# Feed-forward matmuls that stream a chunk's 256 columns in five other orders

## The chip, the cores and the metric

The kernel runs on one core of one Trainium2 chip, as one launch. The metric is device time in microseconds (us) for the whole launch, the median of the runs shown. Nothing else runs beside it: there is no second core, and the host does no arithmetic.

## The reference, cut to what matters

The reference is two transformer blocks in a row on 256 tokens of width 1024. Three of its parts are gated feed-forward layers with 2816 hidden features; the change is made in these three, so only they are shown:

```python
def swiglu(x, w_gate, w_up, w_down):
    return (jax.nn.silu(x @ w_gate) * (x @ w_up)) @ w_down

# first block
f = swiglu(rms_norm(h, ffn1_pre_g[i]), ffn1_w_gate[i], ffn1_w_up[i], ffn1_w_down[i])
h = h + 0.5 * rms_norm(f, ffn1_post_g[i])
...
f = swiglu(rms_norm(h, ffn2_pre_g[i]), ffn2_w_gate[i], ffn2_w_up[i], ffn2_w_down[i])
h = h + 0.5 * rms_norm(f, ffn2_post_g[i])
...
# second block
gate, up = jnp.split(hf @ w_ffn_in[l], 2, axis=-1)
x = x + (jax.nn.silu(gate) * up) @ w_ffn_out[l]
```

Between them stand a mixer with neighbourhood attention and pooling, a per-layer gate, a mixer with stick-breaking attention and a convolution, and attention to a memory. All data are float32.

## The kernel before, in words

Activations lie with features on the 128 partitions and the 256 tokens along the row, so a "chunk" is a tile of 128 features by 256 tokens. Every weight matrix is cut into blocks of 128 x 128, and all blocks come from HBM in one stream, in the order in which they are used: a unit of eight blocks is one DMA (tile `raw`, L63) on the queue of SP.

To come near float32, each operand is split into a high part and a low part of the type float32r: ScalarE writes the high part of a unit (`wh`, L90) and VectorE the low part (`wl`, L101), four units ahead of their use. Activations are split the same way, into two tiles: `xH` and `xL` for the input of a layer, `aH` and `aL` for the hidden features. A product of a block with a chunk is then three matmuls into one PSUM bank, all issued at L184 by way of `mm3`:

```python
self.mm(b, out, w[0], x[0])
self.mm(b, out, w[1], x[0])
self.mm(b, out, w[0], x[1], stop=stop)
```

The weights are the stationary operand (128 columns, loaded by a LDWEIGHTS row of PEld before each matmul), the chunk is the moving operand (256 columns, streamed in a row), and the sum is written to 256 neighbouring words of a PSUM bank.

A feed-forward layer (`ffn`) has two stages. The first makes 22 hidden chunks `m`, each from eight input chunks for the gate and eight for the up half: the first four `m` together, input chunk by input chunk, the other 18 one after the other. The gate half and the up half of one `m` lie side by side in one bank; `evac` multiplies them by the norm's factor (z, L414), takes silu on ScalarE (L415), multiplies (L418) and splits the product into `aH` (ScalarE, L421) and `aL` (VectorE, L424). The second stage makes eight output chunks, each a sum over the 22 hidden chunks. So each of the three layers has 18 x 16 = 288 blocks in the part of the first stage that the change touches, and 8 x 22 = 176 blocks in the second, three matmuls each. What the engines do in which order is written out by hand: `after(n, fn)` and `tick` put small pieces of work of the other engines behind matmuls, and each engine runs its list in order.

Some other lines are spoken of below. `mem_v_task` and `first_group` swap the operands (`mm3t`): there a chunk's 128 tokens are the stationary operand and weights are the moving one, 256 or 512 columns of them, and the first two of the three matmuls have the same stationary operand. L688 (`scaled`, first mixer) reads a bank and the factor with a step of four words and writes in a row; L930 does the same job in the second mixer with everything in a row. L286 (`high_x`) writes `xH`; in the eight calls of the first join it writes with a step of four words (`columns`), elsewhere in a row.

Of the kernel before, what the change touches and what calls it, by code (L numbers as in the profile page):

```python
# [15 lines left out]
P = 128  # L16
# [33 lines left out]
class Stream:  # L50
    """Weight blocks [128, 128] in the order in which the tensor engine takes them."""
# [19 lines left out]
    def split_now(self, u, cuts=(UB,)):  # L71
        """Both parts of unit u, for the start, when nothing else is to be done."""
# [43 lines left out]
def columns(a):  # L116
    """A view of 256 tokens in the order of the grid's columns as one in the order of its rows."""
    return a.rearrange("p (c r) -> p r c", r=GR)


class Bank:
    def __init__(self, t):
        self.t = t
        self.started = False


class Net:
# [63 lines left out]

    def mm3t(self, b, out, x, w, stop=False):
        self.mm(b, out, x[0], w[0])
        self.mm(b, out, x[0], w[1])
        self.mm(b, out, x[1], w[0], stop=stop)

    def proj(self, b, sub, name, m, ks, x):
        """One chunk of 128 outputs, features on partitions."""
        for i, k in enumerate(ks):
            w = self.ws.take(name, k, m)  # L200
            self.mm3(b, b.t[:, sub], w, (x[0][:, k], x[1][:, k]), stop=i == len(ks) - 1)
# [5 lines left out]
    def setup(self):  # L207
# [3 lines left out]
        self.xH = b.tile([P, DC, T], F32R, name="xH")  # L211
        self.xL = b.tile([P, DC, T], F32R, name="xL")
# [33 lines left out]
    def stat(self, parts):  # L246
        """1 / rms of the tokens: parts are pieces [128, 256] of partial sums of squares."""
# [19 lines left out]
    def bcast(self, r):  # L267
        """1 / rms on every partition, in PSUM."""
# [28 lines left out]
    def squares(self, acc, in_, first, scale=1.0):  # L297
        """acc += (scale * in_)^2, chunk by chunk."""
# [8 lines left out]
    def sq_pair(self, j):  # L307
        """Squares of the stream's chunks 2j and 2j + 1."""
# [15 lines left out]
    def post_chunk(self, c, src, gain, scale=1.0):  # L324
        """Chunk c of a branch that is normed before it joins the stream."""
        nc = self.nc
        if c == 0:
            self.acc = self.new_acc()
        self.squares(self.acc, src, c == 0, scale)
        nc.scalar.activation(out=self.fg[:, c], in_=src, func=AF.Copy, scale=gain(c))  # L330

    def join(self, gain, fills, scale=None):
        """h += normed branch; then the next norm's operands, chunk by chunk."""
# [7 lines left out]
        x = (self.xH, self.xL)  # L341
# [43 lines left out]
    def add_chunk(self, c, src, gain, x):  # L385
        """h += branch, with the next norm's operands."""
# [7 lines left out]
    def add_pair(self, j, src, gain, x):  # L394
        """h += branch for two chunks of one bank, with the next norm's operands."""
# [8 lines left out]
    def ffn(self, gate, up, down, on_chunk, nk=4):  # L404
        nc = self.nc
        x = (self.xH, self.xL)
        with self.tc.tile_pool(name="ffn", bufs=1, reuse_waits="tile") as fp:
            self.fp = fp
            aH = fp.tile([P, FC, T], F32R, name="aH")
            aL = fp.tile([P, FC, T], F32R, name="aL")  # L410

            def evac(m, b):
                z = fp.tile([P, 2, T], F32, tag="z", name="z", bufs=6)
                nc.vector.tensor_tensor(out=z, in0=b.t, in1=self.row(rs), op=ALU.mult)  # L414
# [16 lines left out]
            for k in range(DC):  # L431
                for m in range(nk):
                    for sub, (name, off) in enumerate((gate, up)):
                        w = self.ws.take(name, k, off + m)
                        self.mm3(bs[m], bs[m].t[:, sub], w, (x[0][:, k], x[1][:, k]), stop=k == DC - 1)
# [4 lines left out]
            for m in range(nk):  # L440
                evac(m, bs[m])
            for m in range(nk, FC):
                b = self.bank()
                for sub, (name, off) in enumerate((gate, up)):
                    self.proj(b, sub, name, off + m, range(DC), x)
                    if sub == 1:
                        evac(m, b)
                    self.tick()
            for c in range(DC):
                b = self.bank()  # L450
                for k in range(FC):
# [4 lines left out]
                on_chunk(c, b.t[:, 0])  # L456

# [21 lines left out]
    def mem_k_task(self, c):  # L479
        nc = self.nc  # L480
        b = self.bank()
        for k in range(DC):
            w = self.ws.take("w_mem_kv_2", k, c)
            self.mm3(b, b.t[:, 0], w, (self.mH[:, k], self.mL[:, k]), stop=k == DC - 1)
# [29 lines left out]
    def ple_task(self, j):  # L514
        nc = self.nc
        b = self.bank()
        for sub in range(2):
            for k in range(2):
                w = self.ws.take("ple_w_proj", k, 2 * j + sub)
                self.mm3(b, b.t[:, sub], w, (self.pH[:, k], self.pL[:, k]), stop=k == 1)  # L520
# [6 lines left out]
    def first_group(self, win, vc, qc, kc):  # L527
        """Values (tokens on partitions) and the first two chunks of queries and keys, input chunk by chunk."""
        x = (self.xH, self.xL)
        vb = [self.bank() for _ in range(2)]  # L530
        qb = [self.bank() for _ in range(2)]
        for k in range(DC):
# [5 lines left out]
            for i in range(2):  # L538
                for sub, off in enumerate((qc, kc)):
                    w = self.ws.take(win, k, off + i)  # L540
                    self.mm3(qb[i], qb[i].t[:, sub], w, (x[0][:, k], x[1][:, k]), stop=k == DC - 1)
# [6 lines left out]
    def pair_task(self, win, m0, m1, evac):  # L548
        """Two output chunks in one bank; a generator of half tasks."""
        x = (self.xH, self.xL)  # L550
# [17 lines left out]
    def clear_pads(self, qz, vz):  # L568
        """The halves of queries and values that belong to a pair's other head."""
# [25 lines left out]
    def merge(self, tile, na, nb, oa, ob, tg, x, tanh_now):  # L595
        """merged = sigmoid(ga) * branch a + sigmoid(gb) * branch b, split, into x."""
# [25 lines left out]
    def from_merged(self, name, m, on_chunk):  # L622
        bs = [self.bank() for _ in range(2)]
        for ks in (range(DC - 2), (DC - 2, DC - 1)):
            for c in range(4):
                for k in ks:
                    w = self.ws.take(name, k, c)
                    self.mm3(bs[c // 2], bs[c // 2].t[:, c % 2], w, (m[0][:, k], m[1][:, k]), stop=k == DC - 1)
# [13 lines left out]
    def mixer1(self, fills):  # L642
        nc, tc, d = self.nc, self.tc, self.d
        with tc.tile_pool(name="mix1", bufs=1, reuse_waits="tile") as mp:
# [9 lines left out]
            oH = mp.tile([P, 4, T], F32R, name="oH")  # L654
            oL = mp.tile([P, 4, T], F32R, name="oL")
            yH = mp.tile([P, 4, T], F32R, name="yH")
            yL = mp.tile([P, 4, T], F32R, name="yL")
# [78 lines left out]
            def pool_mm(g):  # L736
                b = self.flat_bank()
                w = self.ws.take("pool_w", g, 0)
                self.mm3(b, b.t[:, 0:T], w, (yH[:, g], yL[:, g]), stop=True)
# [82 lines left out]
            m = (self.xH, self.xL)  # L822
# [589 lines left out]
```

## Time and profile before

| what | value |
|---|---|
| device time, median of 2 runs | 1041.83 us (1041.7 to 1041.95) |
| span of the profiled execution, first to last instruction | 1040.2 us |
| granted TensorE clock, mean over the span | 0.998 of full speed |
| matmul rows / weight-load rows | 8606 / 8606 |
| VectorE busy, ScalarE busy | 709.6 us (68%), 545.7 us (52%) |
| HBM traffic over the span | 183 GB/s |

The span is the time of the profiled execution that a trace can show; it lies 1.6 us under the median of the timed runs, for what comes before the first and after the last instruction. A matmul's row begins when it begins to be streamed and its length is modelled and covers the neighbour's start; so what one matmul costs in a dense stretch is read from the distance between the starts of neighbouring rows, not from the rows' lengths.

### The profile page before, as it was taken

What the parts mean: (1) busy time and instruction counts of PE and PEld (TensorE: products, weight loads), DVE (VectorE), ACT (ScalarE), POOL (GpSimd) and SP (SyncE); (2) the same over time, 40 slices, a digit from 0 to 9 for tenths busy, and PEclk for the clock granted to TensorE, in tenths of its full rate; (3) what the DMA queues carried; (4) which work ended last, traced back from release to release, by engine and by line L of the source; (5) the groups of instructions that cost most, each with busy time, mean ns of one, the idle gap of its engine ahead of it and who ended that gap; (6) DMA issues with size and microseconds to landing.
All of it is one profiled execution on the core that took longest, in us unless ns stands there. A gap on an engine that the chain in (4) does not pass through costs nothing.

```text
span 1040.2 us, 20720 instructions
## 1 busy us (share of the span) xinstructions
PE 1030.7 (99%) x8606; PEld 1022.6 (98%) x8606; DVE 709.6 (68%) x1062; ACT 545.7 (52%) x857; POOL 44.0 (4%) x73
## 2 busy tenths in 40 slices
PE   9999999999999999999999999999999999999997
PEld 8999999999999999999999999999999999999996
DVE  7777754587858677666447776886678677666642
ACT  7655544464644555454446565465556555544431
POOL 0100000120000110000000111000001000000000
PEclk9999999999999999999999999999999999999999
DMA  8765564555545655556555666454566346555541
GB/s 287 244 214 181 194 215 171 181 190 185 194 151 166 229 179 193 184 191 190 196 167 177 195 201 194 159 168 157 160 222 226 110 139 219 187 199 182 178 147 42
DMA packets 55023, 191.50 MB, mean 184 GB/s; under 512 B 6400, under 2 KB 7936, under 8 KB 54928
## 3 DMA queue, kind: packets, MB, share of 16 engines
q1 hardware_dynamic: 52992, 184.37, 53.6%
q0 software_dynamic: 1936, 5.80, 1.8%
q8 instruction: 67, 1.10, 0.4%
q14 instruction: 28, 0.23, 0.1%
HBM read 187.00 MB, written 3.15 MB: 183 GB/s over the span
## 4 chain that ended last, share of the span: by engine, by line
PE 81%; issue 16%; DMA 1%; DVE 1%; SPq 0%; POOL 0%; POOLq 0%; DVEq 0%; ACT 0%
PE mm L184 77%; PE at L184 3%; DMA raw<-ws 1%; PE at L839 1%; DMA hg<-gx 0%; DVE sqp L315 0%; POOL r L264 0%; DVE wl L79 0%; SPq L63 0%; DVE wl L101 0%; DVE xL L290 0%; DVE fg L1323 0%; POOLq L1405 0%; DVEq L1405 0%; ACT wh L78 0%
## 5 line engine op out<-in xcount | busy, mean ns | idle before, releaser
L184 PE MATMUL mm<-xH,wh 128*128 128x256 f32 x1760 | 494.9, 281 | 0.0
L184 PE MATMUL mm<-xH,wl 128*128 128x256 f32 x1760 | 492.2, 280 | 0.8 <-DVE wl L79 0.4
L184 PE MATMUL mm<-xL,wh 128*128 128x256 f32 x1760 | 491.4, 279 | 0.0
L101 DVE TENSOR_TENSOR wl<-raw,wh 128x1024 fp32r<-128x1024 f32 x340 | 405.8, 1218 | 22.0 <-ACT wh L90 7.4
L90 ACT CAST wh<-raw 128x1024 fp32r<-128x1024 f32 x340 | 350.2, 1046 | 53.0 <-PE mm L184 33.5
L184 PEld LDWEIGHTS mm<-xH,wl 128*128 128x128 f32 x1760 | 331.2, 188 | 2.6 <-DVE wl L79 1.4
L184 PEld LDWEIGHTS mm<-xH,wh 128*128 128x128 f32 x1760 | 331.3, 188 | 1.6 <-ACT wh L78 0.8
L184 PEld LDWEIGHTS mm<-xL,wh 128*128 128x128 f32 x1760 | 331.1, 188 | 0.0
L184 PE MATMUL mm<-aH,wh 128*128 128x256 f32 x528 | 148.9, 282 | 0.0
L184 PE MATMUL mm<-aL,wh 128*128 128x256 f32 x528 | 148.2, 281 | 0.0
L184 PE MATMUL mm<-aH,wl 128*128 128x256 f32 x528 | 148.2, 281 | 0.0
L415 ACT ACTIVATE z<-z 128x256 f32<-128x256 f32 x66 | 27.2, 418 | 145.6 <-DVE z L414 145.5
L184 PEld LDWEIGHTS mm<-aH,wl 128*128 128x128 f32 x528 | 99.6, 189 | 0.0
L184 PEld LDWEIGHTS mm<-aH,wh 128*128 128x128 f32 x528 | 99.6, 189 | 0.0
L184 PEld LDWEIGHTS mm<-aL,wh 128*128 128x128 f32 x528 | 99.5, 189 | 0.0
L414 DVE TENSOR_TENSOR z<-mm,rs 128x512 f32<-128x512 f32 x66 | 44.7, 689 | 77.5 <-PE mm L184 71.8
L305 DVE TENSOR_TENSOR acc<-acc,sq 128x256 f32<-128x256 f32 x27 | 11.5, 425 | 65.0 <-ACT sq L304 64.9
L264 POOL TENSOR_TENSOR r<-v,mhalf 128x2 f32<-128x2 f32 x13 | 17.6, 1355 | 685.7 <-DVE v L262 685.7
L286 ACT ACTIVATE xH<-hg 128x256 fp32r<-128x256 f32 x48 | 23.6, 543 | 31.9 <-DVE hg L355 22.0
L304 ACT ACTIVATE sq<-mm 128x256 f32<-128x256 f32 x21 | 8.2, 390 | 53.8 <-PE mm L184 53.8
L418 DVE TENSOR_TENSOR z<-z 128x256 f32<-128x256 f32 x66 | 27.2, 423 | 8.7 <-ACT z L415 7.5
L424 DVE TENSOR_TENSOR aL<-z,aH 128x256 fp32r<-128x256 f32 x66 | 26.6, 415 | 0.0
(238 smaller groups left out, 1225.9 us busy)
## 6 DMA issues: line engine op xcount, KB each, us to landing
raw<-ws SPq DMA_DIRECT2D x340, 512.0 KB, 4.1
raw<-ws SPq DMA_DIRECT2D x9, 256.0 KB, 6.0
ub<-ub SPq DMA_DIRECT2D x8, 160.0 KB, 2.9
mraw<-memT POOLq DMA_DIRECT2D x8, 128.0 KB, 3.7
kd<-kv POOLq DMA_DIRECT2D x8, 128.0 KB, 3.0
vd<-kv POOLq DMA_DIRECT2D x4, 256.0 KB, 3.4
kv<-kd POOLq DMA_DIRECT2D x4, 256.0 KB, 6.2
kv<-vd POOLq DMA_DIRECT2D x4, 256.0 KB, 7.1
```

Source lines behind the costliest of these rows:

```text
L90: self.nc.scalar.copy(out=h, in_=self.R[self.nhigh])
L101: self.nc.vector.tensor_tensor(out=l, in0=self.R.pop(u), in1=self.H[u].bitcast(F32), op=ALU.subtract)
L184: self.nc.tensor.matmul(out, lhsT, rhs, start=not b.started, stop=stop, skip_group_check=True)
L264: nc.gpsimd.tensor_tensor(out=r, in0=v, in1=self.mhalf, op=ALU.pow)
L286: self.nc.scalar.activation(out=self.ordered(x[0][:, c]), in_=self.rows(self.h[:, c]), func=AF.Copy, scale=gain(c))
L304: nc.scalar.activation(out=s, in_=in_, func=AF.Square, scale=scale)
L305: nc.vector.tensor_tensor(out=acc, in0=acc, in1=s, op=ALU.add)
L414: nc.vector.tensor_tensor(out=z, in0=b.t, in1=self.row(rs), op=ALU.mult)
L415: nc.scalar.activation(out=z[:, 0], in_=z[:, 0], func=AF.Silu)
L418: nc.vector.tensor_tensor(out=z[:, 0], in0=z[:, 0], in1=z[:, 1], op=ALU.mult)
L424: nc.vector.tensor_tensor(out=aL[:, m], in0=z[:, 0], in1=aH[:, m].bitcast(F32), op=ALU.subtract)
L839: self.nc.tensor.transpose(b.t[:, i * T + t * P:i * T + (t + 1) * P], u[:, t, kt * P:(kt + 1) * P], self.ident)
```

## The change

The high and the low part of an activation now lie in one tile, chunk by chunk: `Split` wraps a tile `[128, chunks, 2, 256]`, and `at(k)` gives the high part, the low part and both in a row (512 columns). All other stages use it with the same three matmuls as before. In the feed-forward layers, from the fifth `m` on and in the whole second stage, the matmuls are issued in other orders:

| layer, stage | order | matmuls |
|---|---|---|
| first, stage 1 | `wide`: high weights over 512 columns in a row (high and low part), low weights over 256; a bank per half | 288 of 512 and 288 of 256 columns |
| first, stage 2 | `(8, 2)`: pairs of words, the next pair 64 bytes on | 528 |
| second, stage 1 | `same`: high weights on the high part, high weights on the low part, then the low weights | 864 |
| second, stage 2 | `(8, 16)`: pieces of 16 words (64 bytes), the next 512 bytes on | 528 |
| third, stage 1 | `(2, 16)`: pieces of 16 words (64 bytes), every second one first | 864 |
| third, stage 2 | `(2, 8)`: pieces of 8 words (32 bytes), every second one first | 528 |

The pieces are taken in the same order from the chunk and in the PSUM bank, so each sum lands where it did. In `wide` the high half of the bank holds two of the three products and the second half the third, so they have to be added: `join2` copies one half to SBUF on ScalarE (L452) and adds the other on VectorE (L453), 36 times each; `evac` then reads `z` from SBUF instead of the bank (L456). Nothing is left out of the computation.

```diff
+class Split:
+    def __init__(self, t):
+        self.t = t
+    def __getitem__(self, i):
+        return self.t[:, :, i]
+    def at(self, k):
+        return self.t[:, k, 0], self.t[:, k, 1], self.t[:, k]
...
+    def mm3o(self, b, out, w, x, order, stop=False):
+        if order == "same":
+            self.mm(b, out, w[0], x[0])
+            self.mm(b, out, w[0], x[1])
+            self.mm(b, out, w[1], x[0], stop=stop)
+            return
+        f = lambda a: a.rearrange("p (a b c) -> p b a c", b=order[0], c=order[1])
+        self.mm3(b, f(out), w, (f(x[0]), f(x[1])), stop=stop)
+
+    def mm2(self, b, w, x, stop=False):
+        self.mm(b, b.t, w[0], x[2])
+        self.mm(b, b.t[:, 0], w[1], x[0], stop=stop)
...
+            def join2(z, b):
+                nc.scalar.copy(out=z, in_=b.t[:, 1])
+                nc.vector.tensor_tensor(out=z, in0=b.t[:, 0], in1=z, op=ALU.add)
...
             for m in range(nk, FC):
-                b = self.bank()
+                z = zt()
                 for sub, (name, off) in enumerate((gate, up)):
-                    self.proj(b, sub, name, off + m, range(DC), x)
-                    if sub == 1:
-                        evac(m, b)
+                    if o1 == "wide":
+                        b = self.bank()
+                        self.wide(b, name, off + m, range(DC), x)
+                        join2(z[:, sub], b)
+                        if sub == 1:
+                            evac(m, z, z)
+                    else:
+                        b = b if sub else self.bank()
+                        for k in range(DC):
+                            self.mm3o(b, b.t[:, sub], self.ws.take(name, k, off + m), x.at(k), o1, stop=k == DC - 1)
...
                 for k in range(FC):
                     w = self.ws.take(down, k, c)
-                    self.mm3(b, b.t[:, 0], w, (aH[:, k], aL[:, k]), stop=k == FC - 1)
+                    if two:
+                        self.mm2(b, w, a.at(k), stop=k == FC - 1)
+                    else:
+                        self.mm3o(b, b.t[:, 0], w, a.at(k), "same" if o2 == "wide" else o2, stop=k == FC - 1)
...
-        self.ffn(("ffn1_w_gate", 0), ("ffn1_w_up", 0), "ffn1_w_down", lambda c, s: self.post_chunk(c, s, gp1))
+        self.ffn(("ffn1_w_gate", 0), ("ffn1_w_up", 0), "ffn1_w_down", lambda c, s, t: self.post_chunk(c, s, gp1, more=t), "wide", (8, 2))
...
+        self.ffn(("ffn2_w_gate", 0), ("ffn2_w_up", 0), "ffn2_w_down", lambda c, s, t: self.post_chunk(c, s, gp2, more=t), "same", (8, 16))
...
+        self.ffn(("w_ffn_in_2", 0), ("w_ffn_in_2", FC), "w_ffn_out_2", self.last_chunk, (2, 16), (2, 8))
```

The case `o2 == "wide"` is in the code but not called, so the added argument of `post_chunk` and `last_chunk` is always empty.

Two places show what moved. The first is TensorE at the end of stage 1 and the beginning of stage 2 of the first layer, before; `x` and `a` are the chunks, `mm` a PSUM bank, and the last figures are the columns of a matmul:

```order
L184 MATMUL mm_1681<-xH_78,wh_1545 128x256
L184 MATMUL mm_1681<-xH_78,wl_1578 128x256
L184 MATMUL mm_1681<-xL_79,wh_1545 128x256
L184 MATMUL mm_1748<-aH_188,wh_1576 128x256
L184 MATMUL mm_1748<-aH_188,wl_1619 128x256
L184 MATMUL mm_1748<-aL_189,wh_1576 128x256
```

The same place now, where three figures behind the 128 are the nested counts of the columns:

```order
L197 MATMUL mm_1518<-x_78,wh_1378 128x512
L197 MATMUL mm_1518<-x_78,wl_1406 128x256
L197 MATMUL mm_1547<-a_186,wh_1404 128x8x16x2
L197 MATMUL mm_1547<-a_186,wl_1441 128x8x16x2
L197 MATMUL mm_1547<-a_186,wh_1404 128x8x16x2 x2
```

A block of stage 1 is two matmuls instead of three, and one of stage 2 is still three, with the columns cut in pairs; the last row joins the third matmul of one block and the first of the next.

The second place is VectorE in stage 1 of the first layer, before:

```order
L101 TENSOR_TENSOR wl_790<-raw_639,wh_750 128x1024
L414 TENSOR_TENSOR z_816<-mm_747,rs_446 128x512
L424 TENSOR_TENSOR aL_189<-z_742,aH_188 128x256
L418 TENSOR_TENSOR z_816<-z_816 128x256
L101 TENSOR_TENSOR wl_826<-raw_681,wh_788 128x1024
L101 TENSOR_TENSOR wl_857<-raw_712,wh_824 128x1024
L414 TENSOR_TENSOR z_883<-mm_821,rs_446 128x512
```

And now:

```order
L101 TENSOR_TENSOR wl_650<-raw_524,wh_612 128x1024
L453 TENSOR_TENSOR z_644<-mm_645,z_644 128x256
L101 TENSOR_TENSOR wl_676<-raw_554,wh_648 128x1024
L453 TENSOR_TENSOR z_644<-mm_671,z_644 128x256
L456 TENSOR_TENSOR z_644<-z_644,rs_443 128x512
L466 TENSOR_TENSOR a_186<-z_582,a_186 128x256
L460 TENSOR_TENSOR z_644<-z_644 128x256
L101 TENSOR_TENSOR wl_706<-raw_584,wh_674 128x1024
L453 TENSOR_TENSOR z_700<-mm_701,z_700 128x256
```

Between two splits of weight units there now stands an addition (L453) that waits for the ScalarE copy of the same half and so for the bank's last matmul; the other work of a chunk is what it was.

## Rows read from the trace of the kernel before

**Rows 1.** The page's totals by engine, and TensorE and its clock in 40 slices

```profile
PE 1030.7 (99%) x8606; PEld 1022.6 (98%) x8606; DVE 709.6 (68%) x1062; ACT 545.7 (52%) x857; POOL 44.0 (4%) x73
...
PE   9999999999999999999999999999999999999997
...
PEclk9999999999999999999999999999999999999999
```

**Rows 2.** Costliest groups: line, engine, operation, count | busy us, mean ns | idle before

```profile
L184 PE MATMUL mm<-xH,wl 128*128 128x256 f32 x1760 | 492.2, 280 | 0.8 <-DVE wl L79 0.4 <-DVE wl L101 0.3
...
L184 PE MATMUL mm<-aH,wh 128*128 128x256 f32 x528 | 148.9, 282 | 0.0
```

**Rows 3.** Timeline of TensorE, first layer, stage 1: start and length, 28 rows

```profile
99.78 0.28 PE L184 MATMUL mm<-xH,wh 128*128 128x256 f32 x1
...
102.93 0.28 PE L184 MATMUL mm<-xH,wh 128*128 128x256 f32 x1
```

**Rows 4.** The same in the first layer's stage 2, 22 rows

```profile
170.03 0.28 PE L184 MATMUL mm<-aH,wl 128*128 128x256 f32 x1
...
172.52 0.28 PE L184 MATMUL mm<-aH,wl 128*128 128x256 f32 x1
```

**Rows 5.** The same in the first mixer, six matmuls of 512 columns

```profile
212.65 0.39 PE L184 MATMUL mm<-wh,xH 128*128 128x512 f32 x1
...
213.81 0.40 PE L184 MATMUL mm<-wh,xL 128*128 128x512 f32 x1
214.05 0.28 PE L184 MATMUL mm<-xH,wh 128*128 128x256 f32 x1
```

**Rows 6.** The same in the memory's values: two matmuls with one stationary operand

```profile
600.71 0.28 PE L184 MATMUL mm<-wh,mH 128*128 128x256 f32 x1
600.83 0.28 PE L184 MATMUL mm<-wl,mH 128*128 128x256 f32 x1
...
602.87 0.28 PE L184 MATMUL mm<-wh,mH 128*128 128x256 f32 x1
```

**Rows 7.** Weight loads of those matmuls: ns min/median/max, first and last start

```profile
L184 PEld LDWEIGHTS mm<-wh,mH x64: 187/188/193, 585.6 to 609.2; 128*128 128x128 f32 x64
...
L184 PEld LDWEIGHTS mm<-wl,mH x64: 187/188/193, 585.7 to 609.4; 128*128 128x128 f32 x64
```

**Rows 8.** VectorE groups by shape: in a row, and (L688) with a step of four words

```profile
L101 DVE TENSOR_TENSOR wl<-raw,wh 128x1024 fp32r<-128x1024 f32 x340 | 405.8, 1218 | 22.0 <-ACT wh L90 7.4 <-issue 7.1 <-PE mm L184 7.1
...
L688 DVE TENSOR_TENSOR tg<-mm,rs 128x512 f32<-128x512 f32 x4 | 4.3, 1077 | 8.9 <-PE mm L184 8.9
...
L566 DVE TENSOR_TENSOR kT<-mm,rs 128x256 f32<-128x256 f32 x8 | 3.4, 424 | 0.1
...
L930 DVE TENSOR_TENSOR tg<-mm,rs 128x512 f32<-128x512 f32 x4 | 2.8, 691 | 8.8 <-PE mm L184 8.8
```

**Rows 9.** ScalarE's writes of xH: ns min/median/max, first and last start

```profile
L286 ACT ACTIVATE xH<-hg x48: 493/509/772, 3.2 to 848.7; 128x256 fp32r<-128x256 f32 x48
L603 ACT ACTIVATE xH<-u x8: 417/417/419, 312.8 to 334.5; 128x256 fp32r<-128x256 f32 x8
...
L1076 ACT CAST xH<-kv x4: 614/618/620, 790.5 to 802.4; 128x512 fp32r<-128x512 f32 x4
```

**Rows 10.** A ScalarE copy of 256 columns out of PSUM

```profile
L276 ACT COPY rs<-at 128x256 f32<-128x256 f32 x6 | 2.2, 372 | 17.4 <-PE at L184 17.4
```

**Rows 11.** Stretches: us, busy PE, PEld, DVE, ACT, POOL with counts, clock, DMA, GB/s

```profile
40.00:140.00 100.00, 100.00 (x858) 100.00 (x858) 73.80 (x110) 53.49 (x89) 3.40 (x6) 1.00 0.61 197
145.00:207.00 62.00, 62.00 (x520) 61.64 (x519) 30.89 (x39) 26.12 (x37) 2.73 (x3) 1.00 0.53 180
385.00:500.00 115.00, 115.00 (x987) 115.00 (x986) 78.45 (x108) 57.80 (x90) 1.08 (x2) 1.00 0.59 191
```

More of the change, by code (lines that the diff above doesn't have):

```diff
@@ L190, in mm3, with wide @@
         self.mm(b, out, w[0], x[1], stop=stop)
+    def mm3o(self, b, out, w, x, order, stop=False):
[9 more added lines that the diff above has]
+        self.mm(b, b.t[:, 0], w[1], x[0], stop=stop)
+    def wide(self, b, name, m, ks, x):
+        for i, k in enumerate(ks):
+            self.mm2(b, self.ws.take(name, k, m), x.at(k), stop=i == len(ks) - 1)
     def mm3t(self, b, out, x, w, stop=False):
@@ L322, in new_acc, with post_chunk @@
         return self.tmp.tile([P, T], F32, tag="acc", name="acc", bufs=2)
-    def post_chunk(self, c, src, gain, scale=1.0):
+    def post_chunk(self, c, src, gain, scale=1.0, more=None):
         nc = self.nc
@@ L328, in post_chunk @@
             self.acc = self.new_acc()
+        if more is not None:
+            nc.scalar.copy(out=self.fg[:, c], in_=more)
+            nc.vector.tensor_tensor(out=self.fg[:, c], in0=src, in1=self.fg[:, c], op=ALU.add)
+            src = self.fg[:, c]
         self.squares(self.acc, src, c == 0, scale)
@@ L340, in join @@
         h, fg = self.h, self.fg
-        x = (self.xH, self.xL)
+        x = self.x
         def mul(lo, n):
@@ L401, in add_pair, with ffn, zt, evac @@
         self.after(3, lambda: self.sq_pair(j))
-    def ffn(self, gate, up, down, on_chunk, nk=4):
+    def ffn(self, gate, up, down, on_chunk, o1, o2, nk=4):
         nc = self.nc
-        x = (self.xH, self.xL)
+        x = self.x
         with self.tc.tile_pool(name="ffn", bufs=1, reuse_waits="tile") as fp:
             self.fp = fp
[L409 to L414, printed above, removed]
+            a = Split(fp.tile([P, FC, 2, T], F32R, name="a"))
+            aH, aL = a[0], a[1]
+            def zt():
+                return fp.tile([P, 2, T], F32, tag="z", name="z", bufs=6)
+            def join2(z, b):
+                nc.scalar.copy(out=z, in_=b.t[:, 1])
+                nc.vector.tensor_tensor(out=z, in0=b.t[:, 0], in1=z, op=ALU.add)
+            def evac(m, z, src):
+                nc.vector.tensor_tensor(out=z, in0=src, in1=self.row(rs), op=ALU.mult)
                 nc.scalar.activation(out=z[:, 0], in_=z[:, 0], func=AF.Silu)
@@ L450, in ffn @@
                 b = self.bank()
+                two = c < DC - 1 and o2 == "wide"
                 for k in range(FC):
                     w = self.ws.take(down, k, c)
-                    self.mm3(b, b.t[:, 0], w, (aH[:, k], aL[:, k]), stop=k == FC - 1)
+                    if two:
+                        self.mm2(b, w, a.at(k), stop=k == FC - 1)
+                    else:
+                        self.mm3o(b, b.t[:, 0], w, a.at(k), "same" if o2 == "wide" else o2, stop=k == FC - 1)
                     if k % 8 == 4:
                         self.tick()
-                on_chunk(c, b.t[:, 0])
+                on_chunk(c, b.t[:, 0], b.t[:, 1] if two else None)
     def mem_prep_chunk(self, c):
@@ L653, in mixer1 @@
             tg2 = mp.tile([P, 4, 2, T], F32, name="tg2")
[L654 to L657, printed above, removed]
+            o = Split(mp.tile([P, 4, 2, T], F32R, name="o"))
+            y = Split(mp.tile([P, 4, 2, T], F32R, name="y"))
+            oH, oL, yH, yL = o[0], o[1], y[0], y[1]
             tg1 = self.fg.rearrange("p (a b) t -> p a b t", b=2)
@@ L1151, in trans @@
                 b = self.transposed(st[h])
-                pH, pL = (mp.tile([P, 2, T], F32R, tag="p" + i, name="p" + i, bufs=n) for i, n in (("H", 2), ("L", 1)))
+                p = Split(mp.tile([P, 2, 2, T], F32R, tag="p", name="p", bufs=2))
+                pH, pL = p[0], p[1]
                 bt = b.t.rearrange("p (a t) -> p a t", a=2)
@@ L1217, in memory, with last_chunk @@
             outk((6, 7), True)
-    def last_chunk(self, c, src):
+    def last_chunk(self, c, src, more):
         nc = self.nc
@@ L1223, in last_chunk @@
         nc.vector.tensor_tensor(out=h[:, c], in0=src, in1=h[:, c], op=ALU.add)
+        if more is not None:
+            nc.vector.tensor_tensor(out=h[:, c], in0=more, in1=h[:, c], op=ALU.add)
         if c == 0:
@@ L1264, in run @@
         mpool = memctx.enter_context(tc.tile_pool(name="memx", bufs=1, side="right"))
-        self.mH = mpool.tile([P, DC, T], F32R, name="mH")
-        self.mL = mpool.tile([P, DC, T], F32R, name="mL")
+        self.m = Split(mpool.tile([P, DC, 2, T], F32R, name="m"))
+        self.mH, self.mL = self.m[0], self.m[1]
         for c in range(DC):
@@ L1307, in run @@
         with tc.tile_pool(name="x2p", bufs=1, side="right", reuse_waits="tile") as xp2:
-            x2 = (xp2.tile([P, DC, T], F32R, name="x2H"), xp2.tile([P, DC, T], F32R, name="x2L"))
+            x2 = Split(xp2.tile([P, DC, 2, T], F32R, name="x2"))
             self.mixer2(x2)
```

73 lines of the change are left out of this document (36 added, 37 removed).

## The prediction

> **What bounds the kernel now.** I read the totals first. TensorE is busy from end to end, its granted clock stands at full speed in every slice, and VectorE and ScalarE have a third and a half of the time free [rows 1]. In the costliest groups the idle time ahead of the 1760 matmuls with low weights is 0.8 us in all, so TensorE practically never waits for weights [rows 2]. The time is therefore the number of matmuls times the distance between their starts, and the change can move it only through that distance, through the number of matmuls, or by making another engine late.
>
> So the distances are what to read. In stage 1 of the first layer 27 steps take 102.93 - 99.78 = 3.15 us, 116.7 ns each [rows 3]; in stage 2, 21 steps take 2.49 us, 118.6 ns each [rows 4]. Matmuls of 512 columns stand 1.40 / 6 = 233.3 ns apart [rows 5]. All three are 0.456 to 0.463 ns per column. [...]
>
> [...] The other engines show what a step costs. VectorE's slope in a row is (691 - 424) / 256 = 1.04 ns per column (L930 against L566); the same operation with a step of four words (L688) takes 1077 - 691 = 386 ns more for 512, so 1.80 ns per element [rows 8]. ScalarE writes xH in a row at (618 - 418) / 256 = 0.78 ns per column; the longest L286 row, which I take for one of the eight with a step of four words, is 772 - 509 = 263 ns over the median, so 0.78 + 1.03 = 1.81 ns per element [rows 9]. With this step each element comes from 16 bytes of its own. TensorE, with four columns in 16 bytes, needs 4 x 0.456 = 1.82 ns for them. [...]
>
> **The change, part by part.** The sums are made against the span of 1040.2 us; the median is 1.6 us more.
>
> Pairs, first layer, stage 2: 528 matmuls. A pair is 8 bytes and the next lies 64 bytes on, so 256 columns touch 128 pieces of 16 bytes where they touched 64. At 1.82 ns each a matmul takes 233 ns, 114.6 more than 118.6, and 528 x 114.6 = +60.5 us. TensorE is the only engine with work to do here (VectorE is busy half of this stretch [rows 11]), so all of it goes on the end. The low bound is 0, if 8 bytes are the unit. The high bound is the rows' price for single elements, 1.82 x 256 = 466 ns, +183 us. I take the middle value, as a pair is one visit to one piece of 16 bytes.
>
> Pieces of 64 and of 32 bytes: 528 + 864 + 528 matmuls. Each piece covers whole 16-byte units (the tiles begin at multiples of 32 bytes by the program's addresses), so the count stays at 64 per matmul: 0. The high bound, if each jump costs one unit more: 16 jumps x 1.82 = 29 ns x (528 + 864) = 40.5 us, and 32 x 1.82 = 58 ns x 528 = 30.8 us, +71 us in all. Nothing in the rows has a jump between whole pieces; I take 0, the end that the unit gives.
>
> 512 in a row, first layer, stage 1: 288 blocks. A block was three times 116.7 = 350 ns and becomes 233.3 + 116.7 = 350 ns: 0. One matmul of three goes and its columns stay. If a saved start were worth the 3 ns by which single distances scatter, it would be -1 us.
>
> Same weights twice, second layer, stage 1: 864 matmuls. The memory's values already have this: the first two of three matmuls share their stationary operand, 18 steps take 2.16 us, 120.0 ns each [rows 6], and each still has its weight load of 188 ns [rows 7]. So nothing is skipped, and as the load doesn't set the distance, skipping it would win nothing: 0, between -1 and +2 us (two ns either way on 864).
>
> The additions of `join2`: 36 copies of 372 ns on ScalarE [rows 10] and 36 additions of 424 ns on VectorE (the L566 row) [rows 8], in a stage of 18 x 5.6 = 101 us. ScalarE goes from 53% to 67%; VectorE from 74% to 74 + 15.3 = 89% [rows 11]. The addition stands in the list ahead of the next weight split and waits for the copy, which waits for the last matmul of the half; behind it are the splits of `wl` (L101), which run four units, 11 us, ahead of TensorE. That cover hides it: 0. Without it, VectorE would have per half of 2.8 us 89% of work and some 0.5 us of waiting, 0.2 us too much, 36 x 0.2 = +7 us. The one tile for both parts adds no wait, since the list of TensorE waits at the same places for ScalarE and VectorE as before.
>
> The sum: 1040.2 + 60.5 + 0 = 1100.7 us of span, 1102 us at the median's distance. With the bounds of the small terms and a unit between 1.7 and 1.9 ns (52 and 66 us), the likeliest case runs from 1092 to 1112 us.
>
> **The rivals.** *Nothing costs anything.* [...] Then a pair is as good as a row, every order gives 116 to 119 ns, and the time is 1041 us, 1038 to 1046. This is the case on the other side, not slower: the mechanism is the width of a fetch in stage 2 of the first layer, its price against my forecast is 60.5 us, and it decides as soon as two neighbouring words suffice. [...]
>
> *Whole pieces cost too, or pairs more than double.* If each jump restarts the stream, the four broken stages take up to 60.5 + 71 = 131 us more, 1173 us; a pair that costs two units alone gives 1041.8 + 183 = 1225 us. From 1115 us on I count it here. For it speaks that PSUM is written in pieces as well, on which the rows have only VectorE's reads; against it that whole pieces leave the number of 16-byte units as it is. [...]
>
> *The pairs cost something, but less than double*, if fetching is partly hidden by the stream's own slack: 10 to 45 us, 1052 to 1088 us.
>
> *VectorE falls behind in `wide`*: +7 us at most as worked out above; it would show inside the other cases and rarely decides one.
>
> [...]
>
> **How the numbers follow.** The likeliest case, 1102 us (1092 to 1112), gets 0.48; nothing costs 0.26; pieces too 0.16; partly 0.07; a relief, or the effect of something not seen, 0.03. A measurement of this kernel tells about 2% from no change, so slower means over 1062.7 us and faster under 1021 us. Slower takes the likeliest, the pieces and nearly all of the partial case: 0.70. Same takes the free case and the rest: 0.28. Faster: 0.02. For 8 in 10 the range has to reach from the free case over the partial one to the likeliest, 0.26 + 0.07 + 0.48 = 0.81: 1038 to 1112 us. Only the pieces' tail and the relief are left out.
>
> **What the profile after would show.** Right: in stage 2 of the first layer the starts stand about 233 ns apart and the stage lasts twice as long, with the clock row at full and VectorE and ScalarE half as busy there; in the five other stages 116 to 119 ns, 350 ns per block in `wide`. A distance of 119 ns under the pairs means that 8 bytes suffice; 145 to 180 under the pieces, that jumps cost; gaps in TensorE's rows ending on L101 in the first layer's stage 1, that VectorE was the one. What would make the prediction wrong is above all the unit: it is read off two other engines.

## The result, and the profile after

The changed kernel takes 1096.93 us (median of 2 runs, 1096.55 to 1097.32) where the kernel before takes 1041.83 us: a ratio of 1.053, with an interval of 1.051 to 1.055. The span of the profiled execution is 1095.6 us, 55.4 us more than before.

The page of the changed kernel, busy time by engine and then the span in 40 slices, answers to [rows 1]:

```profile
PE 1086.0 (99%) x8318; PEld 1059.1 (97%) x8318; DVE 723.2 (66%) x1098; ACT 556.6 (51%) x893; POOL 43.7 (4%) x73
...
PE   9999999999999999999999999999999999999997
...
DVE  7898822228787768766644868786687858666552
ACT  7666622226455465644444656555466646444441
PEclk9999999999999999999999999999999999999999
```

TensorE is as full as before (99% busy both) and its granted clock as high (0.998 both), with 288 matmuls fewer. What stands out is four slices of "2" in VectorE's row, the same in ScalarE's: there the other engines wait for TensorE (from 131.3 to 247 us ScalarE waits 73.2 us for it and VectorE 15.7 us, and VectorE's L337 45.0 us more for ScalarE's L336). Those slices are stage 2 of the first layer, and the list of TensorE's waits in the whole span has none on a matmul of that stage (engine and line that waited, what for, us in total, times, longest):

```profile
PE at L262 <- DVE fg L259: 1.2, 1, 1.2
PE at L197 <- ACT sq L1292: 1.0, 1, 1.0
PE mm L197 <- DVE wl L79: 0.5, 2, 0.3
```

So it isn't waiting but streaming more slowly. The timeline of TensorE in that stage of the changed kernel (start, length; "x2" joins the third matmul of a block and the first of the next) answers to [rows 4]:

```profile
149.75 0.40 PE L197 MATMUL mm<-a,wl 128*128 128x256 f32 x1
149.97 0.62 PE L197 MATMUL mm<-a,wh 128*128 128x256 f32 x2
...
151.73 0.40 PE L197 MATMUL mm<-a,wl 128*128 128x256 f32 x1
```

Between the first and the last row lie three blocks, nine matmuls: 1.98 / 9 = 220.0 ns each, where it was 118.6. One tile's matmuls, stage by stage (ns min/median/max, first and last start): pairs in the first layer's stage 2, then `same`, `(8, 16)`, and `(2, 16)`.

```profile
L197 PE MATMUL mm<-a,wl x176: 396/396/399, 131.3 to 246.8; 128*128 128x256 f32 x176
...
L197 PE MATMUL mm<-x,wh x534: 277/278/281, 444.7 to 538.0; 128*128 128x256 f32 x178
...
L197 PE MATMUL mm<-a,wh x350: 282/283/284, 540.2 to 602.9; 128*128 128x256 f32 x175
L197 PE MATMUL mm<-a,wl x175: 283/283/283, 540.1 to 602.7; 128*128 128x256 f32 x175
...
L197 PE MATMUL mm<-x,wh x540: 282/284/284, 924.9 to 1021.8; 128*128 128x256 f32 x180
L197 PE MATMUL mm<-x,wl x271: 287/287/287, 924.7 to 1021.9; 128*128 128x256 f32 x136
```

How to read them: the first and the last start, divided by the distances between. The pairs: 115.5 / 175 / 3 = 220.0 ns per matmul over the whole stage. `(8, 16)`: 62.8 us over 525 matmuls, 119.8 ns. `(2, 16)`: 97.2 us over 811 matmuls, 120.0 ns. For `same` only the high weights are shown; with the 266 rows of low weights in the same stretch it is 93.3 us over 800 matmuls, 116.8 ns.

For `wide`, a stretch of the first layer's stage 1 in the changed kernel that has nothing else among its matmuls answers to [rows 3, 5]:

```profile
39.68 0.39 PE L197 MATMUL mm<-x,wh 128*128 128x512 f32 x1
39.91 0.28 PE L197 MATMUL mm<-x,wl 128*128 128x256 f32 x1
...
112.83 0.39 PE L197 MATMUL mm<-x,wh 128*128 128x512 f32 x1
```

The rows at 39.68 and 112.83 are 211 blocks apart: 346.7 ns per block, 3.3 ns less than the 350 of three matmuls.

The stretches of the changed kernel, `wide` and pairs (us, busy PE, PEld, DVE, ACT, POOL with counts, clock, DMA share, GB/s), answer to [rows 11]:

```profile
40.00:131.00 91.00, 91.00 (x530) 80.75 (x529) 80.33 (x136) 60.79 (x120) 3.41 (x6) 1.00 0.65 198
131.30:247.00 115.70, 115.70 (x528) 108.34 (x527) 30.83 (x33) 28.19 (x39) 0.00 (x0) 1.00 0.35 108
```

In `wide` VectorE is busy 88% and ScalarE 67% of the stretch. Under the pairs they are busy 27% and 24%, where it was 50% and 42% in the same stage before [rows 11], at a granted clock of 1.00.

The sum by stages, against the distances of before: pairs 528 x (220.0 - 118.7) = +53.5 us; `(2, 16)` 864 x (120.1 - 116.8) = +2.9; `(8, 16)` 528 x (120.0 - 118.7) = +0.7; `wide` 288 x -3.3 ns = -0.9; `same` 0; `(2, 8)` -0.6 (63.58 us from the stage's first start to its last, 64.22 before). Together +55.6 us, and the span shows +55.4. These are differences between stages; no run sets the `(2, 16)` stage alone back to a row, so that its +2.9 us come from the pieces is not shown.

### The profile page after: what moved, and what is told of

It is laid out like the page before. It is cut to its first block, busy times and chain, and to the rows that moved or that the text cites. A ratio compares the mean times of both kernels' runs of the same rounds, so it can differ in the third digit from the quotient of the medians.

```text
span 1095.6 us, 20201 instructions
## 1 busy us (share of the span) xinstructions
PE 1086.0 (99%) x8318; PEld 1059.1 (97%) x8318; DVE 723.2 (66%) x1098; ACT 556.6 (51%) x893; POOL 43.7 (4%) x73
## 4 chain that ended last, share of the span: by engine, by line
PE 83%; issue 16%; DMA 0%; SPq 0%; DVE 0%; POOL 0%; POOLq 0%; DVEq 0%; ACT 0%
PE mm L197 79%; PE at L197 3%; PE at L893 0%; DMA raw<-ws 0%; POOL r L296 0%; SPq L63 0%; SPq L254 0%; DVE fg L1380 0%; POOLq L1462 0%; DVE wl L79 0%; DVEq L1462 0%; ACT wh L78 0%; DVE v L294 0%
## 5 line engine op out<-in xcount | busy, mean ns | idle before, releaser
L197 PE MATMUL mm<-x,wh 128*128 128x256 f32 (+1 forms) x3360 | 655.7, 291 | 0.2
L197 PEld LDWEIGHTS mm<-x,wh 128*128 128x128 f32 x3360 | 529.0, 188 | 13.2 <-ACT wh L78 1.2
L197 PE MATMUL mm<-x,wl 128*128 128x256 f32 x1824 | 512.9, 281 | 0.6 <-DVE wl L79 0.5
L101 DVE TENSOR_TENSOR wl<-raw,wh 128x1024 fp32r<-128x1024 f32 x340 | 407.2, 1219 | 45.4 <-PE mm L197 22.3
L197 PEld LDWEIGHTS mm<-x,wl 128*128 128x128 f32 x1824 | 343.4, 188 | 2.2 <-DVE wl L79 1.4
L197 PE MATMUL mm<-a,wh 128*128 128x256 f32 x1056 | 236.0, 321 | 0.0
L197 PEld LDWEIGHTS mm<-a,wh 128*128 128x128 f32 x1056 | 181.8, 195 | 5.0
L197 PE MATMUL mm<-a,wl 128*128 128x256 f32 x528 | 169.3, 321 | 0.0
L197 PEld LDWEIGHTS mm<-a,wl 128*128 128x128 f32 x528 | 102.9, 195 | 2.4
L456 DVE TENSOR_TENSOR z<-mm,rs 128x512 f32<-128x512 f32 x48 | 32.3, 689 | 62.5 <-PE mm L197 55.9
L337 DVE TENSOR_TENSOR acc<-acc,sq 128x256 f32<-128x256 f32 x27 | 11.5, 426 | 93.7 <-ACT sq L336 93.7
L336 ACT ACTIVATE sq<-mm 128x256 f32<-128x256 f32 x21 | 8.2, 392 | 81.4 <-PE mm L197 81.4
L318 ACT ACTIVATE x<-hg 128x256 fp32r<-128x256 f32 x56 | 27.4, 537 | 43.1 <-DVE hg L391 22.0
L197 PE MATMUL mm<-y,wh 128*128 128x256 f32 x136 | 27.8, 283 | 0.0
```

Of the source, the lines that this page charges most:

```text
L101: self.nc.vector.tensor_tensor(out=l, in0=self.R.pop(u), in1=self.H[u].bitcast(F32), op=ALU.subtract)
L197: self.nc.tensor.matmul(out, lhsT, rhs, start=not b.started, stop=stop, skip_group_check=True)
L318: self.nc.scalar.activation(out=self.ordered(x[0][:, c]), in_=self.rows(self.h[:, c]), func=AF.Copy, scale=gain(c))
L337: nc.vector.tensor_tensor(out=acc, in0=acc, in1=s, op=ALU.add)
L456: nc.vector.tensor_tensor(out=z, in0=src, in1=self.row(rs), op=ALU.mult)
```

## The experiments

Where a result is one run, the numbers are the distances in its trace; the mean granted clock of these traces is 0.996 to 0.998, so they can be compared with each other.

**1. The pairs taken back.** Is the whole loss in one stage, or partly in the other orders and in the combined tile? Only the order of the first layer's stage 2 is changed, to the three matmuls in a row as before:

```diff
-        self.ffn(("ffn1_w_gate", 0), ..., "wide", (8, 2))
+        self.ffn(("ffn1_w_gate", 0), ..., "wide", "plain")
```

> The changed kernel with only the pairs undone: the first layer's stage 2 streams its columns in a row again; the other five stages keep their new orders. If the pairs are the whole loss (528 matmuls x 101.3 ns = 53.5 us, from 220.0 ns after against 118.7 before), this runs at 1096.9 - 53.5 = 1043.4 us. If the pieces or the additions carry part of the loss, it stays above 1047 us; if the small gains of 512 in a row outweigh them, it falls under 1041.

Measured: 1044.09 us (1043.8 to 1045.18, 9 runs) against 1041.84 us, a ratio of 1.0023 (1.0013 to 1.0032). TensorE on the hidden features in that stage:

```profile
L197 PE MATMUL mm<-a,wh x299: 282/283/283, 140.9 to 194.5; 128*128 128x256 f32 x150
```

The last of them starts at 194.5 us instead of 247.0. So the pairs are the whole loss but for about 2 us, which the small terms of the sum above account for: without the pairs' 53.5 they make 2.1, and this stage, 120.0 ns in a row out of the combined tile, adds 0.7. The two profiled spans differ by 2.8 us, 1043.0 against 1040.2.

**2. The read or the write?** The pairs are taken from SBUF and put in PSUM in the same order, so either side could be the slow one. Here the first layer's stage 2 reads pairs and writes PSUM in a row; the second layer's stage 2 reads in a row and writes pairs, 64 bytes apart. The ScalarE copy of each sum restores the order of the columns.

```diff
-        self.mm3(b, f(out), w, (f(x[0]), f(x[1])), stop=stop)
+        if order[2:] != ("sbuf",):
+            out = f(out)
+        if order[2:] != ("psum",):
+            x = f(x[0]), f(x[1])
+        self.mm3(b, out, w, x, stop=stop)
...
-        ... "wide", (8, 2))
+        ... "wide", (8, 2, "sbuf"))
-        ... "same", (8, 16))
+        ... "same", (8, 2, "psum"))
```

> Pairs on one side only, all else as in the changed kernel. First layer, stage 2: the chunk is read in pairs, the PSUM bank is written in a row (ScalarE puts the columns back in order when it empties the bank). Second layer, stage 2: the chunk is read in a row, the bank is written in pairs. My theory, that SBUF is fetched 16 bytes at a time: about 220 ns per matmul in the first layer's stage 2 and 119 in the second's, total near 1096 us. Rival, that PSUM's writes are what a pair costs: 119 ns in the first and 220 in the second, total near 1096 us as well. If either side alone is enough, 220 in both and about 1149 us; if both sides are needed, 119 in both and 1043 us.

Measured: 1097.47 us (one run). The two stages, the read in pairs first:

```profile
L197 PE MATMUL mm<-a,wl x175: 396/396/399, 131.7 to 246.6; 128*128 128x256 f32 x175
...
L197 PE MATMUL mm<-a,wh x351: 277/281/283, 540.6 to 602.9; 128*128 128x256 f32 x176
```

Pairs from SBUF: 114.9 / 174 / 3 = 220 ns. Pairs into PSUM: 62.3 us for 526 matmuls, 118.7 ns, nothing at all. The cost is on the read of the moving operand, shown.

**3. What is the unit?** Call it a visit when a piece takes columns out of one aligned unit of 16 bytes. If each visit has its price, pairs 16 bytes apart must cost as much as pairs 64 bytes apart, and pieces of four words nothing.

```diff
-        ... "wide", (8, 2))      # first layer
-        ... "same", (8, 16))     # second
-        ... (2, 16), (2, 8))     # third
+        ... "wide", (2, 2))
+        ... "same", (16, 4))
+        ... (64, 2), (2, 8))
```

> Other cuts of the columns, both sides alike, all else as in the changed kernel. First layer, stage 2: pairs whose neighbour lies 16 bytes on instead of 64. Second layer, stage 2: pieces of 4 words, 16 bytes, with 256 bytes from one to the next. Third layer, stage 1: pairs that hop 512 bytes each time. My theory (each visit to 16 bytes costs 1.72 ns, whatever the way between): 220, 118 to 120 and 220 ns per matmul; total 1096.9 + 864 x 100 ns = 1183 us. Rival, that the step decides (places in SBUF that get in each other's way): the pairs at 16 and at 512 bytes differ from 220 and from each other by over 15 ns. Rival, that each jump costs a fixed 0.79 ns (101 ns for 128 jumps): the 4-word pieces with 64 jumps take 118.7 + 51 = 170 ns.

Measured: 1156.75 us (one run), where the theory said 1183. Pairs 16 bytes apart (first layer, stage 2), four words 256 bytes apart (second layer, stage 2), then pairs taken in turn from the two halves of a row, 512 bytes apart (third layer, stage 1):

```profile
L197 PE MATMUL mm<-a,wl x161: 405/407/408, 141.7 to 251.5; 128*128 128x256 f32 x161
...
L197 PE MATMUL mm<-a,wh x351: 295/302/304, 545.1 to 616.5; 128*128 128x256 f32 x176
...
L197 PE MATMUL mm<-x,wh x576: 346/346/405, 932.8 to 1082.5; 128*128 128x256 f32 x192
```

Pairs 16 bytes apart: 109.8 / 160 / 3 = 228.8 ns, near the 220 of the unit. Four words: 71.6 us from the first start of 528 matmuls to the last, 135.8 ns, where the unit says 118 to 120 and a fixed price per jump 170; neither holds. Alternating pairs: 149.7 us for 864 matmuls, 173.4 ns, where both say 220. The rival of the step has one of its two: the alternating pairs are more than 15 ns off 220, the pairs at 16 bytes are not. So the unit alone doesn't give every number, and the next run goes on with distances.

**4. The distance of the hop.** All stages that the change touches get pairs or pieces of four words, with hops of 32 to 512 bytes.

```diff
+        ... (2, 4), (4, 2))      # first layer
+        ... (8, 4), (16, 2))     # second
+        ... (32, 4), (32, 2))    # third
```

> The same cuts with other distances, in all six stages. Pairs in the three stages 2, the next pair 32, 128 and 256 bytes on; pieces of 4 words in the three stages 1, the next 32, 128 and 512 bytes on. Known so far: pairs at 16 and 64 bytes 229 and 220 ns, pairs that alternate between two places 512 bytes apart 173; 4 words at 256 bytes 136; in a row 117 to 119. If each visit to 16 bytes costs the same wherever it is, the pairs take 220 to 229 ns at all three distances and the 4 words 117 to 120 at all three (or 136, if any jump costs a little), and the 173 and 136 stay unexplained. If the distance decides (two visits overlap when they lie far enough apart), pairs at 32 and 128 bytes stay near 220 and those at 256 come down towards 173, and the 4 words differ by over 10 ns. Total by the first: near 1200 us; by the second: 1170 to 1200 us.

Measured: 1230.52 us (one run), over both forecasts. Pairs 32 bytes apart (first layer, stage 2), then four words 32 bytes apart (first layer, stage 1) and 512 bytes apart (third layer, stage 1):

```profile
L197 PE MATMUL mm<-a,wl x176: 412/412/413, 132.9 to 255.4; 128*128 128x256 f32 x176
...
L197 PE MATMUL mm<-x,wh x425: 280/282/284, 39.9 to 114.8; 128*128 128x256 f32 x142
...
L197 PE MATMUL mm<-x,wh x570: 292/293/293, 989.9 to 1098.0; 128*128 128x256 f32 x190
```

Four words, with the rows of low weights, 638 and 855 matmuls: 117.9 and 126.8 ns; with hops of 128 bytes 123.7. Pairs: 122.5 / 175 / 3 = 233.3 ns at 32 bytes, 224.1 at 128, 225.8 at 256. Neither forecast holds as it stands: the pairs at 256 bytes don't come down towards 173, and three numbers lie outside the ranges of a price that is the same everywhere. From 16 to 256 bytes the hop moves the pairs by 6% (220 to 233 ns), and up to 512 bytes it moves the four words by 15% (117.9 to 135.8), with no order in it; whether a piece has two words or four makes nearly the factor of two. The pairs that alternate between two places are the exception.

**5. Where a piece begins.** If aligned units of 16 bytes are what counts, and not the number of pieces, then pieces of four words that begin in the middle of a unit must cost as much as pairs. The tile of the hidden features gets four words more and begins two words later in the first layer.

```diff
-            a = Split(fp.tile([P, FC, 2, T], F32R, name="a"))
+            o2, n = o2 if type(o2[0]) is tuple else (o2, 0)
+            a = fp.tile([P, FC * 2 * T + 4], F32R, name="a")[:, n:n + FC * 2 * T]
+            a = Split(a.rearrange("p (c e t) -> p c e t", c=FC, e=2))
...
+        ... (8, 2), ((8, 4), 2))       # first layer
+        ... (32, 2), ((8, 4), 0))      # second
+        ... (4, 2), ((1, 2), 0))       # third
```

> Where pieces begin. Second layer, stage 2: pieces of 4 words, 128 bytes from one to the next, each on a 16-byte boundary. First layer, stage 2: the same pieces with the whole tile moved by 8 bytes, so that each piece lies in two pieces of 16 bytes. Third layer, stage 2: columns in a row, but named as 128 runs of 2. Stages 1: pairs at 64, 256 and 32 bytes on the other tile. If 16 bytes are fetched as one: the moved pieces take 220 ns or more against 118 to 136 for the aligned ones, and the row named in pairs 117 to 119. If the number of pieces decides and not where they lie: moved and aligned within 5 ns. If the nested form of the counts is what costs: the row named in pairs takes 200 ns or more.

Measured: 1383.89 us (one run). The same pieces, 128 bytes apart, moved by two words (first layer) and not moved (second layer):

```profile
L197 PE MATMUL mm<-a,wl x176: 403/409/413, 222.2 to 339.1; 128*128 128x256 f32 x176
...
L197 PE MATMUL mm<-a,wl x176: 280/282/296, 727.4 to 790.5; 128*128 128x256 f32 x176
```

116.9 / 175 / 3 = 222.7 ns against 63.1 / 175 / 3 = 120.2 ns: the same columns, the same hops, only 8 bytes further on. So where a piece begins counts, and not only how many pieces there are: the aligned unit of 16 bytes is shown. The third layer's stage 2 settled nothing: its pattern of 128 runs of two was passed on as one row of 256 (117.7 ns). The pairs in the first stages gave 221.2 (hop 64 bytes), 226.7 (256) and 233.4 ns (32).

**6. Pairs across a boundary.** Moved by one word, every second pair lies in two units. A simple count gives 64 + 2 x 64 = 192 visits, some 330 ns.

```diff
+        ... (1, 4), ((8, 2), 1))       # first layer
+        ... (16, 4), ((1, 256), 1))    # second
+        ... (16, 2), ((64, 2), 0))     # third
```

> Odd starts. First layer, stage 2: pairs at 64 bytes with the tile moved by 4 bytes, so that every second pair... lies across an 8-byte boundary, all within 16 bytes or across them as their place has it (word 1 and 2 of four). Second layer, stage 2: columns in a row, tile moved by 4 bytes. Third layer, stage 2: pairs alternating 512 bytes apart, on the other tile than before. Stages 1: a row named in runs of 4 words, 4 words at 256 bytes, pairs at 128 bytes. If 16 bytes are fetched as one: pairs of words 1 and 2 lie within one piece of 16 bytes and cost the same 220 ns as before, and the moved row 117 to 121. If 8 bytes are the unit: each such pair takes two fetches, 300 ns and over, and the moved row stays. The alternating pairs repeat 173 ns if the distance is the cause and the tile is not; the row in runs of 4 stays at 117.

Measured: 1235.89 us (one run). The pairs moved by a word, first layer, stage 2:

```profile
L197 PE MATMUL mm<-a,wl x176: 401/409/417, 131.9 to 250.9; 128*128 128x256 f32 x176
```

119.0 / 175 / 3 = 226.7 ns, 3% more than the 220.0 inside units and far from 330: crossing costs next to nothing on top, and the simple count fails here. The expectation spoke of pairs inside a unit and overlooked that half of them cross; with them in view, the number suggests that a visit for one column isn't paid in full. The second layer's stage 2 has a row that begins one word off:

```profile
L197 PE MATMUL mm<-a,wl x176: 280/281/284, 558.5 to 622.1; 128*128 128x256 f32 x176
```

63.6 / 175 / 3 = 121.1 ns, where a row on a boundary took 120.0 (experiment 1): a start off a boundary costs a row almost nothing. Alternating pairs take 164.6 ns in the first 105 matmuls on the hidden features and 168 over the stage (173.4 on the input chunks), four words 256 bytes apart on the input chunks 133.4 (135.8): what experiment 3 found odd is there again. Pairs at 128 bytes on the input chunks take 226.7 ns. The row named in runs of four (first layer, stage 1) was passed on as one row of 256, 116.7 ns, and settled nothing.

**7. Counting.** Moved pieces of 4, 8 and 16 words touch 128, 96 and 80 units. That gives three points on one line, and rivals that part from it.

```diff
+        ... (8, 8), ((8, 8), 2))       # first layer
+        ... (8, 16), ((8, 16), 2))     # second
+        ... (16, 8), ((8, 4), 3))      # third
```

> Second stages read the hidden features from a tile that is moved by some words; first stages are controls with whole, aligned pieces. Count theory (a matmul costs the number of 16-byte units that its pieces touch, counted anew for each piece, times 1.72 to 1.82 ns, and no less than 117 ns): first layer, stage 2, pieces of 8 words moved by 8 bytes, 3 units each, 96 in all, 165 to 175 ns; second layer, stage 2, pieces of 16 words moved by 8 bytes, 5 units each, 80 in all, 138 to 146 ns; third layer, stage 2, pieces of 4 words moved by 12 bytes (one word and three words of two units), 128 in all, 220 to 233 ns. Rival A (whatever begins off a 16-byte boundary in pieces runs at half speed throughout): 220 to 227 ns in all three. Rival B (columns are read two at a time, and a read is free if it lies wholly in the unit in which the one before it ended): 165 to 175 and 138 to 146 as the count, but 117 to 125 in the third layer, since the second read of a piece lies in the unit in which the first ended. Controls, aligned pieces of 8 and 16 words on the input chunks: 117 to 124 ns in all theories (pieces of 4 words with the same hops gave up to 136). Whole: count 1126 to 1150 us, rival A 1195 to 1215, rival B 1075 to 1090.

Measured: 1154.84 us (one run). Stage 2 of the first, the second and the third layer (of the third, the part up to 1088 us):

```profile
L197 PE MATMUL mm<-a,wl x176: 342/342/363, 137.3 to 228.7; 128*128 128x256 f32 x176
...
L197 PE MATMUL mm<-a,wl x176: 316/318/322, 525.0 to 602.1; 128*128 128x256 f32 x176
...
L197 PE MATMUL mm<-a,wl x94: 396/397/399, 1025.6 to 1087.5; 128*128 128x256 f32 x94
```

91.4 / 175 / 3 = 174.1 ns for 96 units (1.81 each), 77.1 / 175 / 3 = 146.9 ns for 80 (1.84 each), 61.9 / 93 / 3 = 221.9 ns for 128 (1.73 each). Rival A, half speed for whatever is moved, falls in the first two stages; rival B, a second read that is free, in the third. The count has two of its three in the forecast and the third at 146.9 just over the 138 to 146. The controls, aligned pieces of 8 and 16 words, took 122.3, 120.1 and 123.4 ns, inside their 117 to 124; on 864 matmuls each that is 13 us more than at 116.8, and the whole came out 5 us over its 1126 to 1150.

**8. The order that saves time, in all six stages.** `wide` was the only order below 350 ns per block. Here it stands in both stages of all three layers; the case `o2 == "wide"` of stage 2 adds the second half of the bank in the copy that follows; the last output chunk takes the order `same`.

```diff
+        ... "wide", "wide")      # all three layers
```

> 512 in a row in both stages of all three layers (in stage 2 for seven of the eight output chunks; the eighth uses the same weights twice). In the changed kernel's first layer a wide block takes 228 + 118 = 346 to 348 ns against 3 x 116.7 = 350 before. If a saved start is worth that much everywhere, stage 1 gains 2.7 x 288 x 3 = 2.3 us and stage 2, whose three matmuls took 356 ns, 8 to 10 ns x 154 x 3 = 3.7 to 4.6 us against the kernel before: about 1035 us. Rival, that the gain is only in how the rows lie and stage 2's slower distance stays (237 + 119 ns): 1039 to 1042 us. Rival, that the copies and additions make VectorE late in a stage: over 1043 us, with gaps in TensorE's rows.

Measured: 1035.0 us (1034.52 to 1035.76, 5 runs) against 1041.84, a ratio of 0.9936 (0.9924 to 0.9949). That is 0.6% under the kernel before: clear of the scatter, but within the 2% below which two kernels count as the same. The first layer's stage 2:

```profile
181.69 0.39 PE L197 MATMUL mm<-a,wh 128*128 128x512 f32 x1
181.92 0.28 PE L197 MATMUL mm<-a,wl 128*128 128x256 f32 x1
182.04 0.39 PE L197 MATMUL mm<-a,wh 128*128 128x512 f32 x1
...
182.73 0.39 PE L197 MATMUL mm<-a,wh 128*128 128x512 f32 x1
```

Three blocks in 1.04 us, 347 ns, where three matmuls of 118.7 took 356. In the second stages that is 9 ns on 3 x 154 blocks, 4.2 us; in the first stages 3.3 ns on 864, 2.9 us; 7.1 us in all, and the span is 6.6 us shorter. VectorE goes to 73%, and TensorE's only wait for it is the 1.2 us of L262, which the kernel before has too (L230):

```profile
PE 1024.8 (99%) x7280; PEld 964.2 (93%) x7280; DVE 758.1 (73%) x1191; ACT 585.1 (57%) x979; POOL 44.9 (4%) x73
```

## Why the prediction was right, step by step

- *The bound.* TensorE's distances were the place to look: the whole change of the span is the sum of distances times counts, to 0.2 us.
- *Pairs.* The mechanism held for the pairs that were forecast, and its size was off: the term was 114.6 ns on 528 matmuls, +60.5 us, and it measured 101.3 ns, +53.5 us. The step that was mis-sized is the price of a visit, 1.82 ns, read off VectorE and ScalarE and off TensorE's own row; at 64-byte hops TensorE visits in 220.0 / 128 = 1.72 ns. At 32-byte hops it is 233.3 / 128 = 1.82. The bounds given for that price, 1.7 and 1.9 ns, hold both. That TensorE is paced by such visits was the author's estimate; the 102.5 ns between moved and aligned pieces in experiment 5 are the measurement that bears it out. That a price of other engines holds for TensorE was a guess that came out; no run shows why they should agree. And a price for every visit is not the whole rule. It would give the crossing pairs of experiment 6 some 330 ns at 1.72 ns each (226.7 measured) and the alternating pairs of experiment 3 220 (173.4).
- *Which side.* The prediction priced the pieces of 16 bytes that the columns touch, and of PSUM's writes it had no row. Experiment 2 shows that it is SBUF alone: 220 ns with the pairs on the read, 118.7 with the pairs on the write.
- *"Nothing costs".* By this rival the pairs were free and the time 1041 us; the pairs take 220 ns. Experiment 5 moves whole pieces by 8 bytes, half of 16, and goes from 120.2 to 222.7 ns. Two neighbouring words don't suffice: a pair is two words of one unit of 16 bytes and takes 220 ns per matmul against 118.7.
- *"Whole pieces cost too".* This was the rival behind the 71 us. `(2, 16)` goes with 2.9 us, `(8, 16)` with 0.7, `(2, 8)` with none; the 0.7 is no more than a row out of the combined tile shows in experiment 1 (120.0 ns both). Nor does a broken write to PSUM slow the matmuls in experiment 2: pairs into PSUM stand 118.7 ns apart.
- *Wide.* 346.7 ns per block against 350: the small gain named as the bound ("-1 us") is what came, -0.9. A relief of the stream by an order, which is in the prediction's 0.03, was shown no larger than this: 3.3 ns of 350 per block here, 9 ns of 356 in experiment 8, and 0.6 us over the whole stage of `(2, 8)`.
- *Same weights twice.* 116.8 ns before and after, and still one weight load for each matmul (8318 and 8318); nothing is saved by the order.
- *join2.* VectorE was forecast at 89% and ScalarE at 67%, and measured at 88% and 67%; no row of TensorE waits on L101, so the copy and the addition are hidden.

One of the three readings behind the 1.82 ns was high. The ScalarE row of 772 ns is the longest of the eight that write with a step of four words, and their median is 742 (ns min/median/max):

```profile
L286 ACT ACTIVATE xH<-hg x8: 706/742/772, 203.0 to 214.1; 128x256 fp32r<-128x256 f32 x8
```

With 742 in place of 772 that reading becomes 0.78 + (742 - 509) / 256 = 1.69 ns.

Shown are the side, the aligned unit, and that for whole pieces and moved pieces the time goes with the number of units (64 units 117 to 120 ns in a row and in most pieces, 80 units 147, 96 units 174, 128 units 220 to 233). Argued only: that no more than one visit is paid for two columns. It would give the crossing pairs' 226.7 ns and agrees with all moved pieces. What stays open: why alternating pairs take 165 to 173 ns, the 122 to 136 ns of some whole pieces at certain hops, and the 1 to 3 ns between tiles in a row. Single words, where a visit for each column would part from one for two, weren't tried.

## What to carry to other kernels

Let the moving operand of a matmul (float32r here) come out of SBUF in runs of at least four words that begin on 16-byte boundaries: 117 to 136 ns for 256 columns. Runs of two through four or more places (220 to 233 ns), or four words half a unit off (222.7), nearly double the matmul, while TensorE's busy share (99%), its clock (1.00 in the stage) and its waits (none on a matmul of the stage) look healthy. If the columns must change places, do it on the PSUM side, where pairs 64 bytes apart cost nothing here (118.7 ns). Where both parts of a split operand lie in a row, streaming them as one matmul of 512 columns saves 3 to 9 ns per block; with the added copies and additions hidden the span fell by 6.6 us (experiment 8).

## What the hardware showed that was not expected

- Writing PSUM in pairs 64 bytes apart costs what a row costs: 118.7 ns both.
- A matmul can stream at close to half speed (220 ns for 256 columns) with the granted clock at 1.00: the row of the clock doesn't show it, only the distance between starts does, and beside it VectorE and ScalarE, busy 27% and 24% of the stage instead of 50% and 42%.
- Going back and forth between two places 512 bytes apart is cheaper for pairs (165 to 173 ns) than going through four or more places (224 to 227 ns at 128 and 256 bytes).
- Eight bytes in the start of a tile can be worth 102 ns per matmul (120.2 against 222.7 ns).
